# The last forgetting-attention pair sends three query tiles through DRAM, and the cross attention's first two query-weight loads queue behind the mixer's output weights

## The chip, the cores and the metric

The kernel runs on one core of one Trainium2 chip. The metric is the device time of one execution in microseconds (us), the median of several runs; lower is better. Engines are named as in the profile: PE is TensorE (matrix multiply; PEld is its weight load), DVE is VectorE, ACT is ScalarE, POOL is GpSimd, SP is SyncE, which here only issues DMAs; SPq is its queue.

## What is computed

One layer of a streaming encoder over 512 tokens of width 1024, in float32. A mixer runs four branches from one projection of the normalized input (differential attention, forgetting attention, a Conformer convolution, a short gated convolution), weighs them with sigmoid gates and projects the sum; then cross attention into 256 memory tokens; then a gated feed-forward block. The change touches the forgetting attention and the loading of the cross attention's query weights:

```python
def _forgetting_attention(q, k, v, log_f, t_pos):
    ...
    c = jnp.cumsum(log_f.astype(jnp.float32), axis=1)
    ...
        s = jnp.einsum('bqhd,bkhd->bhqk', q_blk, k, preferred_element_type=jnp.float32) * scale
        s = s + c_blk[..., None] - c_k[:, :, None, :]
        mask = t_pos[None, :] <= tq_blk[:, None]
        p = jax.nn.softmax(jnp.where(mask, s, -jnp.inf), axis=-1)
        return jnp.einsum('bhqk,bkhd->bqhd', p.astype(v.dtype), v)
...
        mixed = jnp.sum(gates * proj, axis=2) @ w_out[l]
        x = x + _rms_norm(mixed, norm_mix_post[l])
        hx = _rms_norm(x, norm_x_pre[l])
        ...
        xq = (hx @ w_xq[l]).reshape(B, S, X_HEADS, X_HEAD_DIM)
```

## The kernel before

**Arithmetic.** Every float32 product is made of three matmuls on a high part and a low part of each operand (`mm3`): high by high, high by low, low by high. So each weight block that arrives in the buffer `wr` is cast to `wh` on ACT (L201), and the rest is subtracted into `wl` on DVE (L202). `wr` has two buffers, `wh` and `wl` four each.

**Order of the work.** `run_blocks` takes a list of jobs in a fixed order (each is a weight load and a body of matmuls) and fetches the weights of later jobs ahead of the current one. The attention pieces are generators on a background queue (`bg`), which are advanced between the matmuls of the jobs. The instructions recorded in this way are then reordered on each engine by a list scheduler that works with estimated durations; an engine executes its own list strictly in order, and waits at an instruction until what that one needs has arrived.

**Forgetting attention.** The eight heads are worked in four pairs, `f_task(p, ...)` with p from 0 to 3. A pair has four steps for its query tiles of 128 tokens, tile 0 to tile 3, with 128, 256, 384 and 512 keys. In a step, POOL makes the forget bias, PE makes the scores of both heads into banks named `ps_sc` (`scores`), DVE adds the bias and takes the smallest (L1123; L1130 after the change), ACT takes the exponentials, and DVE and ACT scale them into the tile `e`, with queries on partitions. For the product with the values the keys have to be on partitions instead, in the tiles `pth` (high part) and `ptl` (low part). There are two ways to turn them:

- *through DRAM* (pairs 0 to 2): DVE transposes 32 x 32 squares (`turn_squares`, L857), SP writes the result to a DRAM tile `turned` (`put`, L862), and two more DMAs, one for each head, bring it back rearranged into `ptl` (`get`, L869). `split_in_place` then makes the high part on ACT (L875) and the low part on DVE (L876).
- *by the identity* (pair 3): PE transposes each 128 x 128 block against an identity matrix into a bank `ps_tr` (`to_keys_major`, L250), and `split` copies it from there with ACT (L164) and DVE (L165).

Tiles 0 and 1 together make the first half of the product with the values (`values(..., half=0)`), tiles 2 and 3 the second half; both accumulate into a bank `ps_av` for each head. The outcome goes into `y["f"]`. Around pair 3 the jobs on PE are the gate and branch blocks of the forgetting branch (`gate_blocks(1, "f", ...)`): gate blocks `ps_mm<-hth,wh` need nothing of the pair; the branch blocks `ps_mm<-y,wh` sum over four slices of `y["f"]`, of which the fourth is pair 3's.

**Mixer output and cross attention.** `mix_out_jobs` multiplies with seven products instead of eight and loads its weights (`load_parts`, L591) first into `wr`, then into a four-slot tile `wide`. The query weights of the cross attention, `in_w_xq`, are loaded by the job list's ordinary `load_weights` (L185) into `wr`; they are first needed when the mixer's output has been normalized.

Of the kernel before, what the change touches and what calls it, by code (L numbers as in the profile page):

```python
# [18 lines left out]
F32R = mybir.dt.float32r  # L19
# [6 lines left out]
P = 128  # L26
S = 512
# [11 lines left out]
HALF_SHIFT = 16  # L39
# [47 lines left out]
def hybrid_layer(ctx: ExitStack, tc: tile.TileContext, a: dict, out: bass.AP):  # L87
# [21 lines left out]
    def share_now(*among):  # L109
        vars(turn_of).update(n=1, among=among)  # L110
# [102 lines left out]
    steps_of = []  # L213
# [374 lines left out]
    def load_parts(raw, parts):  # L588
        c = 0
        for x in parts:  # L590
            SP.dma_start(raw[:, c:c + x.shape[1]], x)  # L591
            c += x.shape[1]

    def activation_sums(x, z, eng):
# [16 lines left out]
    def y8(dtype=F32R):  # L611
        return m2p.tile([P, 4, S], dtype, tag="y8", name="y8", bufs=2)
# [255 lines left out]
    def get(d, n, pt, local):  # L868
        SP.dma_start(part_of(pt[1], n, local).bitcast(F32), d.rearrange("(a j) (b x) -> (j b) a x", j=32, b=4))  # L869

    def split_in_place(n, pt, local):
        hi, lo = (part_of(x, n, local) for x in pt)
        raw = lo.bitcast(F32)
        with tc.issue_after(evacuations[0]):
            A.copy(hi, raw)  # L875
        V.tensor_tensor(lo, raw, hi.bitcast(F32), ALU.subtract)  # L876
# [21 lines left out]
    def pt_tiles():  # L898
        return tuple(m1p.tile([P, 2, 4, 4, 32], F32R, tag=n, name=n, bufs=2) for n in ("pth", "ptl"))
# [152 lines left out]

    def f_task(p, qk, v):
        f_steps[p] = 0
        far = p < 3
        while f_steps[p - 1] < 4:
            yield 0.0, 0.5
        ck = []
        for j in range(2):
            t = m1p.tile([P, S], F32, tag="ck", name="ck", bufs=2)  # L1060
            G.dma_start(t, crows[2 * p + j:2 * p + j + 1, :].rearrange("a s -> (a s)").partition_broadcast(P))
            ck.append(t)
        yield 0.0, 2.0 if p else 5.0
        es, pts, av, ready = {}, None, None, []
# [8 lines left out]
        for step in range(8 if far else 6):  # L1073
            if step in ((5, 7) if far else (3, 5)):
                if av is None:
                    av = [bank("av"), bank("av")]
                with tc.issue_after(steps_of[0]) if far else ExitStack():
                    for j in range(2):
                        hl = v[0][:, :, 2 * p + j]
                        values(av[j], lambda kt: ((hl[:, kt], 0), (hl[:, kt], 1)), pts[j],  # L1080
                               step // 2 - (2 if far else 1))
            while step == (3 if far else 2) and f_steps[p - 1] < 8:
                yield 0.0, 0.5
            f_steps[p] = step + 1
            cost = 0.0
            if step == 4:
                turn_ready()
            if far:
                for qt in SPLITS.get(step, ()):
                    for j in range(2):  # L1090
                        split_in_place(qt + 1, pts[j], qt % 2)
                    cost += 0.1 + 0.3 * qt
                for qt in GETS.get(step, ()):
                    if qt % 2 == 0:
                        pts = [pt_tiles() for _ in range(2)]
                    d = es.pop(qt)
                    for j in range(2):
                        get(d[:, j], qt + 1, pts[j], qt % 2)
            else:
                if step == 2:  # L1100
                    share_now("mm")
                for qt in {2: (0, 1), 3: (2,), 4: (3,)}.get(step, ()):
                    if qt % 2 == 0:
                        pts = [pt_tiles() for _ in range(2)]
                    e = es.pop(qt)
                    for j in range(2):
                        to_keys_major(e[:, j], qt + 1, pts[j], qt % 2)
                    cost += 0.4 + 0.3 * qt
            if step < 4:
                qt, w = step, (step + 1) * P  # L1110
                e = es[qt] = e4()
                st = m1p.tile([P, 8], F32, tag="st8", name="st8", bufs=4)
                for j in range(2):
                    head = 2 * p + j
                    bias = m1p.tile([P, S], F32, tag="fbias", name="fbias", bufs=2)

                    G.tensor_scalar(bias[:, :w], ck[j][:, :w], -1.0, cq[:, qt, head:head + 1],  # L1117
                                    ALU.mult, ALU.add)
                    G.affine_select(out=bias[:, w - P:w], in_=bias[:, w - P:w], pattern=[[-1, P]],
                                    compare_op=ALU.is_ge, fill=BIG, base=0, channel_multiplier=1)  # L1120
                    ps = bank("sc")
                    scores(ps, qk, j, qt * P, w)
                    low = V.tensor_tensor_reduce(e[:, j, :w], ps[:, :w], bias[:, :w], scale=-HD ** -0.5,  # L1123
                                                 scalar=3.0e38, op0=ALU.add, op1=ALU.min,
                                                 accum_out=st[:, j:j + 1])
# [12 lines left out]
                if far:  # L1138
                    ready.append((qt, e, w))
                    cost += 0.003 * w  # L1140
            yield cost, 6.5 if far and step == 5 else 4.5
        if "f" not in y:
            y["f"] = (y8(), y8())

        e = e4()
        for j in range(2):
            A.copy(e[0:HD, j], av[j][HD:P])
# [386 lines left out]
    def xq_jobs():  # L1534
        held = []
        for h in range(4):
            def body(hi, lo, h=h):
                held.append((hi, lo))

                def part(h, half):  # L1540
                    sl = slice(half * 256, (half + 1) * 256)
                    ps = bank()
                    (channel_major if h else by_pass)(ps, held[h], ns.hx, sl)
                    split(ps[:, sl], ns.xq[0][:, h, sl], ns.xq[1][:, h, sl])
                    bg.add(cross_task(h, half), f"x{half}")
                    bg.tick()

                if h == 0:
                    bg.drain("n0")
                part(h, 0)  # L1550
                if h == 3:
                    bg.drain("n1")
                    for g in range(4):
                        part(g, 1)
            yield *cols(w_xq, h * P), body, V, same, HALF_SHIFT

    def cross_values(half):
        bg.drain(f"x{half}")
# [333 lines left out]
```

## Time and profile before

| | |
|---|---|
| median of 3 runs | 1044.31 us (1044.2 to 1044.91) |
| the profiled execution, its own time | 1043.87 us |
| its span in the trace | 1042.1 us |
| TensorE clock granted | 0.999 |
| instructions | 14386 |
| PE, DVE, ACT, POOL busy | 1032.0, 816.3, 511.0, 158.5 us |

The busy times are unions of the intervals in which an engine had an instruction under way. Matmuls overlap: a new one starts before the one ahead has ended, so what one costs PE is read from the distance between starts and not from its duration. All times below are microseconds from the start of the span, unless ns is said.

### The profile page before, as it was taken

Reading aid. Unit: us, or ns where it says so; the run is one execution under the profiler, and the core shown is the slowest. Engines: PE = TensorE matmul, PEld = TensorE weight load, DVE = VectorE, ACT = ScalarE, POOL = GpSimd, SP = SyncE. Lnnn points to the kernel's source line nnn. Section 1 sums busy time; section 2 is a strip of 40 time slices with the busy share of each in tenths; the row PEclk is TensorE's granted clock in tenths of the full one; section 3 lists DMA queues with packets and bytes.
Section 4 is the critical chain, followed back from the end, with each engine's and each line's share of the span. In section 5 each row is a group of like instructions: output and inputs, shape, how many; then the busy total and the mean of one; then the engine's idle time right before and its main releaser. Section 6 shows DMA issues by size and latency. Waiting matters only on the chain.

```text
span 1042.1 us, 14386 instructions
## 1 busy us (share of the span) xinstructions
PE 1032.0 (99%) x5201; PEld 877.1 (84%) x5201; DVE 816.3 (78%) x1257; ACT 511.0 (49%) x838; POOL 158.5 (15%) x235
## 2 busy tenths in 40 slices
PE   9999999999999999999999999999999999999997
PEld 7888888888888988888888899998888888888886
DVE  7999999577788668878487898776767777667796
ACT  5322222376566365666444666655333433445662
POOL 4001000100020214353011031121112121111012
PEclk9999999999999999999999999999999999999999
DMA  8954333334534346766348744135577676625662
GB/s 268 311 159 104 102 101 101 84 99 115 148 104 126 90 130 169 199 175 161 104 136 284 246 127 121 59 123 181 187 241 235 211 234 210 218 81 186 212 218 82
DMA packets 190141, 167.79 MB, mean 161 GB/s; under 512 B 22079, under 2 KB 161708, under 8 KB 190069
## 3 DMA queue, kind: packets, MB, share of 16 engines
q1 hardware_dynamic: 181027, 135.11, 43.6%
q10 hardware_dynamic: 6482, 23.21, 6.2%
q0 software_dynamic: 2560, 8.54, 2.6%
q8 instruction: 41, 0.67, 0.3%
q14 instruction: 31, 0.25, 0.1%
HBM read 141.39 MB, written 25.44 MB: 160 GB/s over the span
## 4 chain that ended last, share of the span: by engine, by line
PE 96%; DMA 2%; DVE 1%; ACT 0%; issue 0%; POOL 0%; POOLq 0%; DVEq 0%; SPq 0%; ACTq 0%
PE ps_mm L244 46%; PE ps_av L244 30%; PE ps_tr L244 11%; PE ps_sc L244 7%; PE ps_tr L250 1%; DMA ptl<-turned 1%; PE ps_mm L462 1%; PE ps_av L462 1%; DMA turned<-e 0%; DMA xs<-in_x 0%; DVE e L857 0%; DVE e L939 0%; PE ps_tr L446 0%; DVE wl L202 0%; DVE o L1782 0%
## 5 line engine op out<-in xcount | busy, mean ns | idle before, releaser
L201 ACT CAST wh<-wr 128x1024 fp32r<-128x1024 f32 (+1 forms) x140 | 146.4, 1047 | 235.4 <-PE ps_mm L244 121.1
L202 DVE TENSOR_TENSOR wl<-wr,wh 128x1024 fp32r<-128x1024 f32 (+1 forms) x140 | 174.9, 1250 | 83.3 <-ACT wh L201 82.5
L244 PE MATMUL ps_mm<-hth,wh 128*128 128x512 f32 (+1 forms) x536 | 198.6, 378 | 0.0
L244 PE MATMUL ps_mm<-htl,wh 128*128 128x512 f32 (+1 forms) x536 | 198.4, 377 | 0.0
L244 PE MATMUL ps_mm<-hth,wl 128*128 128x512 f32 (+1 forms) x536 | 198.1, 377 | 0.0
L244 PE MATMUL ps_av<-htl,wh 128*128 128x512 f32 (+1 forms) x328 | 122.5, 373 | 0.0
L244 PE MATMUL ps_av<-hth,wh 128*128 128x512 f32 (+1 forms) x328 | 122.5, 374 | 0.0
L244 PE MATMUL ps_av<-hth,wl 128*128 128x512 f32 (+1 forms) x328 | 122.3, 373 | 0.0
L244 PEld LDWEIGHTS ps_mm<-hth,wl 128*128 128x128 f32 x536 | 99.1, 188 | 18.3
L244 PEld LDWEIGHTS ps_mm<-hth,wh 128*128 128x128 f32 x536 | 99.0, 188 | 18.1 <-ACT hth L164 0.3
L244 PEld LDWEIGHTS ps_mm<-htl,wh 128*128 128x128 f32 x536 | 98.9, 188 | 17.8
L697 DVE SCALAR_TENSOR_TENSOR y<-y,par,y 128x508 f32<-128x508 f32 (+29 forms) x120 | 82.6, 727 | 0.1
L244 PEld LDWEIGHTS ps_av<-hth,wh 128*128 128x128 f32 x328 | 61.6, 188 | 11.2 <-DVE e L1148 0.3
L244 PEld LDWEIGHTS ps_av<-hth,wl 128*128 128x128 f32 x328 | 61.6, 188 | 11.0
L244 PEld LDWEIGHTS ps_av<-htl,wh 128*128 128x128 f32 x328 | 61.6, 188 | 10.7
L1683 DVE TENSOR_TENSOR wl<-dw,wh 128x1024 fp32r<-128x1024 f32 x32 | 40.1, 1259 | 17.2 <-ACT wh L1682 17.1
L1682 ACT CAST wh<-dw 128x1024 fp32r<-128x1024 f32 x32 | 33.5, 1051 | 24.7 <-PE ps_tr L244 8.2
L1630 ACT ACTIVATE th<-c 128x512 f32<-128x512 f32 x22 | 13.9, 632 | 48.6 <-DVE c L624 48.6
L1117 POOL TENSOR_SCALAR fbias<-ck,cq 128x128 f32<-128x128 f32 (+3 forms) x32 | 24.2, 763 | 64.2 <-DVE st L1123 55.9
L624 DVE SCALAR_TENSOR_TENSOR c<-ps_mm,par,c 128x510 f32<-128x510 f32 (+1 forms) x44 | 32.7, 744 | 0.7
L244 PE MATMUL ps_tr<-htl,wh 128*128 128x512 f32 x80 | 31.7, 396 | 0.0
L244 PE MATMUL ps_tr<-hth,wh 128*128 128x512 f32 x80 | 31.6, 396 | 0.0
(514 smaller groups left out, 2242.2 us busy)
## 6 DMA issues: line engine op xcount, KB each, us to landing
wr<-in_w_up SPq DMA_DIRECT2D x44, 512.0 KB
wr<-in_w_in SPq DMA_DIRECT2D x38, 512.0 KB
wr<-in_w_gate SPq DMA_DIRECT2D x32, 512.0 KB
wp<-in_w_down ACTq DMA_DIRECT2D x22, 512.0 KB
sums<-wp ACTq DMA_DIRECT2D x22, 512.0 KB
dw<-sums SPq DMA_DIRECT2D x44, 256.0 KB
wr<-in_w_branch SPq DMA_DIRECT2D x16, 512.0 KB
wide<-in_w_out SPq DMA_DIRECT2D x12, 512.0 KB
```

The costliest lines, as they stand in the source:

```text
L201: last_weights[:] = [order(A.copy(hi, raw[:, :n])).ins, low.tensor_tensor(lo, raw[:, :n], hi.bitcast(F32), ALU.subtract).ins]
L202: low.tensor_tensor(lo, raw[:, :n], hi.bitcast(F32), ALU.subtract).ins]
L244: steps_of[:] = [PE.matmul(ps, lhs, rhs, start=start, stop=stop).ins]
L250: turns.append(PE.transpose(ps, x, ident[:n, :n]).ins)
L462: keep(PE.matmul(banks[c][:, :S // 2], w[p == 1][:, k, c * P:(c + 1) * P], ht[p == 2][:, i * 4 + k, :S // 2], start=(i, p, k) == (0, 0, 0) ...
L624: ins = V.scalar_tensor_tensor(dst[:, s:], src[:, :S - s], w(k), dst[:, s:], ALU.mult, ALU.add)
L697: ins = V.scalar_tensor_tensor(dst[:, s:], src[:, :S - s], pc("conv_dw", k * 4 + j), dst[:, s:], ALU.mult, ALU.add)
L1117: G.tensor_scalar(bias[:, :w], ck[j][:, :w], -1.0, cq[:, qt, head:head + 1], ALU.mult, ALU.add)
L1630: A.activation(th, c[:, 0], AF.Silu)
L1682: A.copy(hi, x)
L1683: V.tensor_tensor(lo, x, hi.bitcast(F32), ALU.subtract)
```

## The change

Pair 3 now sends its query tiles 0, 1 and 2 through DRAM, as the other pairs do, and turns only tile 3 by the identity. Tiles 0 and 1 return into a new tile `half` (`own_tiles`), which takes the buffer of an earlier pair's `qk`. Its steps are 0 to 6, with the first half of the values at step 5 and the second at step 6. `y["f"]` is allocated at the start of the first pair instead of at its end. In `xq_jobs`, the first two loads of `in_w_xq` are put behind the last DMA that `load_parts` has issued (`ns.part`), which is the last of the mixer's output weights.

```diff
     def load_parts(raw, parts):
...
-            SP.dma_start(raw[:, c:c + x.shape[1]], x)
+            ns.part = SP.dma_start(raw[:, c:c + x.shape[1]], x).ins
...
     def f_task(p, qk, v):
         f_steps[p] = 0
-        far = p < 3
+        last = p == 3
...
+        if "f" not in y:
+            y["f"] = (y8(), y8())
+        es, pts, av, ready = {}, {}, None, []
+        gets, splits, rests, ends = ({4: (2,)}, {4: (0, 1), 5: (2,)}, {3: 2.0}, (5, 6)) if last else (GETS, SPLITS, {5: 6.5}, (5, 7))
+
+        def fetch(qt):
+            d = es.pop(qt)
+            for j in range(2):
+                get(d[:, j], qt + 1, pts[qt // 2][j], qt % 2)
+
+        def own_tiles():
+
+            free = m1p.tile([P, 6, S], F32R, tag="qk", name="half", bufs=2)
+            return [tuple(free[:, 2 * j + i].rearrange("p (l a t i) -> p l a t i", l=2, a=4, t=2) for i in range(2))
+                    for j in range(2)]
...
-            if far:
-                for qt in SPLITS.get(step, ()):
...
-            else:
-                if step == 2:
-                    share_now("mm")
-                for qt in {2: (0, 1), 3: (2,), 4: (3,)}.get(step, ()):
...
-                        to_keys_major(e[:, j], qt + 1, pts[j], qt % 2)
+            for qt in splits.get(step, ()):
+                for j in range(2):
+                    split_in_place(qt + 1, pts[qt // 2][j], qt % 2)
+                cost += 0.1 + 0.3 * qt
+            for qt in gets.get(step, ()):
+                if qt % 2 == 0:
+                    pts[qt // 2] = [pt_tiles() for _ in range(2)]
+                fetch(qt)
+            if step == 4 and last:
+                share_now("mm")
+                e = es.pop(3)
+                for j in range(2):
+                    to_keys_major(e[:, j], 4, pts[1][j], 1)
+                cost += 1.3
...
-                if far:
+                if not last or qt < 3:
                     ready.append((qt, e, w))
                     cost += 0.003 * w
+                if last and qt == 2:
+                    pts[0] = own_tiles()
+                    fetch(0)
+                    fetch(1)
...
     def xq_jobs():
...
-            yield *cols(w_xq, h * P), body, V, same, HALF_SHIFT
+            def load(h=h):
+                with tc.issue_after(ns.part) if h < 2 else ExitStack():
+                    raw = load_raw(*cols(w_xq, h * P))
+                return split_weights(*raw, V, same, HALF_SHIFT)
+
+            yield load, None, body
```

What the scheduler makes of it is seen in the order of the instructions. On PE, before, pair 3's transposes of the third query tile stand between gate blocks (`ps_mm`) and pair 2's products with the values (`ps_av<-pth,v`):

```order
L244 MATMUL ps_av<-ptl,v 128x256
L244 MATMUL ps_av<-pth,v 128x128
L244 MATMUL ps_av<-ptl,v 128x128
L250 MATMUL ps_tr_4698<-ident,e 128x128 x3
L244 MATMUL ps_mm<-hth,wh 128x512
L244 MATMUL ps_mm<-htl,wh 128x512
L244 MATMUL ps_mm<-hth,wl 128x512
L244 MATMUL ps_av<-pth,v 128x256
```

After, on PE, only the eight transposes of the fourth tile are left. They stand behind 33 gate matmuls that follow the last scores, and the products with `half` (query tiles 0 and 1) stand among them:

```order
L244 MATMUL ps_mm<-hth,wl 128x512
L250 MATMUL ps_tr_4728<-ident,e 128x128 x4
L244 MATMUL ps_av<-half,v 128x256 x2
L250 MATMUL ps_tr_4721<-ident,e 128x128 x4
L244 MATMUL ps_av<-half,v 128x128 x2
L244 MATMUL ps_av<-half,v 128x256 x2
L244 MATMUL ps_av<-half,v 128x128 x2
L244 MATMUL ps_mm<-hth,wh 128x512
```

The second half of the values follows 15 matmuls later: six of the gate block and nine of a branch block. Twelve transposes have left PE's list.

On SP, before, nothing but weight loads follows the last two returns of pair 2 (128x4x128):

```order
L869 DMA ptl<-turned 128x4x128 x2
L185 DMA wr<-in_w_gate 128x8x128
L185 DMA wr<-in_w_branch 128x4x256
L185 DMA wr<-in_w_gate 128x8x128 x2
L185 DMA wr<-in_w_branch 128x4x256
```

After, on SP, three write-outs and six returns of pair 3 stand among them:

```order
L869 DMA ptl<-turned 128x4x128 x2
L862 DMA turned<-e 128x2x128
L185 DMA wr<-in_w_gate 128x8x128
L869 DMA half<-turned 128x4x32 x2
L862 DMA turned<-e 128x2x256
L185 DMA wr<-in_w_branch 128x4x256
L869 DMA half<-turned 128x4x64 x2
L862 DMA turned<-e 128x2x384
L869 DMA ptl<-turned 128x4x96 x2
L185 DMA wr<-in_w_gate 128x8x128 x2
```

A weight load that stood right behind another one now stands behind a return, which cannot be issued before the write-out ahead of it has landed.

Further on in SP's list, before, the first two loads of `in_w_xq` stand among the loads of the mixer's output weights (`wide`):

```order
L185 DMA wr<-in_w_xq 128x8x128
L591 DMA wide<-out_sums 128x512 x2
L591 DMA wide<-in_w_out 128x512
L591 DMA wide<-out_sums 128x512 x3
L591 DMA wide<-in_w_out 128x512
L591 DMA wide<-out_sums 128x512
L185 DMA wr<-in_w_xq 128x8x128
```

After, on SP, both stand behind the last of these and ahead of the cross attention's key and value weights (`mix<-in_w_xkv`):

```order
L591 DMA wide<-in_w_out 128x1024 x2
L591 DMA wide<-out_sums 128x512 x2
L185 DMA wr<-in_w_xq 128x8x128 x2
L185 DMA mix<-in_w_xkv 128x8x128 x3
L185 DMA mix<-in_w_xkv 128x2x512 x4
```

Both loads have moved past all the `wide` loads, and seven of the eight `in_w_xkv` loads now stand behind them. In the mixer's output projection and everything behind it PE's list is the same in both kernels, and so are those of DVE, ACT and POOL.

More of the change, by code (lines that the diff above doesn't have):

```diff
@@ L1072, in turn_ready @@
                 es[qt] = put(turned, w)
-        for step in range(8 if far else 6):
-            if step in ((5, 7) if far else (3, 5)):
+        for step in range(ends[1] + 1):
+            if step in ends:
                 if av is None:
                     av = [bank("av"), bank("av")]
-                with tc.issue_after(steps_of[0]) if far else ExitStack():
+                with tc.issue_after(steps_of[0]):
                     for j in range(2):
                         hl = v[0][:, :, 2 * p + j]
-                        values(av[j], lambda kt: ((hl[:, kt], 0), (hl[:, kt], 1)), pts[j],
-                               step // 2 - (2 if far else 1))
-            while step == (3 if far else 2) and f_steps[p - 1] < 8:
+                        half = ends.index(step)
+                        values(av[j], lambda kt: ((hl[:, kt], 0), (hl[:, kt], 1)), pts[half][j], half)
+            while step == (4 if last else 3) and f_steps[p - 1] < 8:
                 yield 0.0, 0.5
@@ L1087, in f_task @@
                 turn_ready()
-            if far:
-                for qt in SPLITS.get(step, ()):
[L1090 to L1098, printed above, removed]
-            else:
-                if step == 2:
-                    share_now("mm")
-                for qt in {2: (0, 1), 3: (2,), 4: (3,)}.get(step, ()):
[L1103 to L1106, printed above, removed]
-                        to_keys_major(e[:, j], qt + 1, pts[j], qt % 2)
-                    cost += 0.4 + 0.3 * qt
+            for qt in splits.get(step, ()):
[12 more added lines that the diff above has]
+                cost += 1.3
             if step < 4:
@@ L1137, in f_task @@
                 cost += 0.6 + 0.0038 * w
-                if far:
+                if not last or qt < 3:
                     ready.append((qt, e, w))
                     cost += 0.003 * w
-            yield cost, 6.5 if far and step == 5 else 4.5
-        if "f" not in y:
-            y["f"] = (y8(), y8())
+                if last and qt == 2:
+                    pts[0] = own_tiles()
+                    fetch(0)
+                    fetch(1)
+            yield cost, rests.get(step, 4.5)
         e = e4()
```

1 line of the change is left out of this document (removed).

## The prediction

> **What bounds the kernel now.** I read the page first: the busy shares, then the chain of work that ended last; then the view of who PE waited for.
>
> ```profile
> PE 1032.0 (99%) x5201; PEld 877.1 (84%) x5201; DVE 816.3 (78%) x1257; ACT 511.0 (49%) x838; POOL 158.5 (15%) x235
> PE 96%; DMA 2%; DVE 1%; ACT 0%; issue 0%; POOL 0%; POOLq 0%; DVEq 0%; SPq 0%; ACTq 0%
> PE ps_mm L403 <- DVE e L353: 1.3, 1, 1.3
> PE ps_tr L446 <- DVE nt L441: 1.0, 1, 1.0
> PE ps_av L244 <- ACT pth L875: 0.7, 1, 0.7
> ```
>
> PE is busy for 99% of the span and carries 96% of the chain. The last three rows are all the waits of PE that the trace names (in total, how often, the longest): two belong to the kernel's first lines, and the only one in the middle is 0.7 us, for the product with the values of an earlier task. So a change in the middle of this kernel is worth what it takes off PE's list, less what PE must newly wait for. Nothing that is saved on another engine counts by itself.
>
> **What leaves PE.** Tiles 0, 1 and 2 have 1, 2 and 3 blocks of keys, for two heads: 12 transposes. Their price is read from the starts of the rows around them in PE's timeline (start, duration, then the operation):
>
> ```profile
> 496.68 0.38 PE L250 MATMUL ps_tr<-ident,e 128*128 128x128 f32 x2
> 496.82 0.48 PE L244 MATMUL ps_mm<-hth,wh 128*128 128x512 f32 x1
> 497.14 0.40 PE L244 MATMUL ps_mm<-htl,wh 128*128 128x512 f32 x1
> 497.38 0.39 PE L244 MATMUL ps_mm<-hth,wl 128*128 128x512 f32 x1
> ...
> 503.04 0.52 PE L250 MATMUL ps_tr<-ident,e 128*128 128x128 f32 x3
> 503.31 0.48 PE L244 MATMUL ps_mm<-hth,wh 128*128 128x512 f32 x1
> ```
>
> Two transposes hold the next start back by 0.14 us, three by 0.27. The matmul right behind them takes 0.32 us to the next start (496.82 to 497.14), where the one after it takes 0.24 (to 497.38) and most of its kind 0.23, so a group costs some 0.09 us more for what follows it. The groups are: tile 0 with both heads in one place ahead of the scores, where I count 0.14 alone; tile 1 twice two, 2 x 0.23 = 0.46; tile 2 twice three, 2 x 0.36 = 0.72. In sum **1.3 us less on PE**. Tile 3's eight transposes stay.
>
> [...]
>
> **What DVE, ACT and SP get instead.** DVE loses six subtractions out of `ps_tr` and gets six transposes of squares and six subtractions in place; ACT keeps as many casts. SP gets three write-outs and six returns.
>
> ```profile
> 500.00:505.00 5.00, 5.00 (x30) 4.29 (x29) 2.12 (x3) 2.84 (x6) 0.00 (x0) 1.00 0.36 105
> 484.96 0.37 SPq L185 DMA_DIRECT2D wr<-in_w_gate  x1
> 498.98 1.04 ACT L201 CAST wh<-wr 128x1024 fp32r<-128x1024 f32 x1
> ```
>
> The first row is a stretch of 5 us in the view by stretches (PE, PEld, DVE, ACT, POOL busy, then clock, DMA share and GB/s): DVE is busy for 2.12 us of it and ACT for 2.84, so the added work lies beside PE's. What is queued behind the returns on SP are weight loads, and a return waits for its write-out first. The other two rows show why that is covered: with two buffers `wr`, the load issued at 484.96 is cast only at 498.98, 14 us later, and the cast weights then wait in one of four buffers. A load that comes 5 us late still comes in time. Without this cover each wait on SP would be PE time in full.
>
> **The new wait.** What can reach PE is the round trip of tiles 1 and 2, because the new order gives the products with them fixed places in PE's list. These rows give its parts: SP's issues of a write-out (L862) and of the return (L869) that waited for it; the first casts behind a return; and the steps around them:
>
> ```profile
> 395.46 1.06 SPq L862 DMA_DIRECT2D turned<-e  x1
> 399.07 0.92 SPq L869 DMA_DIRECT2D ptl<-turned  x2
> 400.51 0.36 SPq L862 DMA_DIRECT2D turned<-e  x1
> 403.25 0.91 SPq L869 DMA_DIRECT2D ptl<-turned  x2
> ...
> 460.44 0.37 SPq L862 DMA_DIRECT2D turned<-e  x1
> 461.42 0.62 SPq L869 DMA_DIRECT2D ptl<-turned  x1
> 465.74 0.91 SPq L869 DMA_DIRECT2D ptl<-turned  x2
> 402.27 0.58 ACT L875 CAST pth<-ptl 128x128 fp32r<-128x128 f32 x2 [2.77 <-DMA ptl<-turned]
> 466.50 0.75 ACT L875 CAST pth<-ptl 128x128 fp32r<-128x128 f32 x2 [1.41 <-DMA ptl<-turned]
> 465.82 1.60 DVE L857 STREAM_TRANSPOSE e<-e 128x384 f32<-128x384 f32 x2 [0.25 <-DMA turned<-e]
> 489.43 0.55 DVE L1123 CUSTOM_DVE_ANT_0 e<-ps_sc,fbias 128x384 f32<-128x384 f32 x1
> 492.90 0.65 POOL L1119 TENSOR_SCALAR_AFFINE_SELECT fbias<-fbias 128x128 f32<-128x128 f32 x2
> 492.25 1.15 PE L244 MATMUL ps_sc<-qk 128*128 128x512 f32 x4
> 493.24 0.40 PE L244 MATMUL ps_mm<-hth,wh 128*128 128x512 f32 x1
> ```
>
> A write-out takes 3.6 us (395.46 to 399.07), 2.7 (400.51 to 403.25) or 5.3 (460.44 to 465.74, with returns in flight beside it). A return takes about 3.2 us (399.07 to 402.27) or 5.1 (461.42 to 466.50).
>
> *When PE wants the tiles.* The scores of tile 3 start at 492.25 in before. Now 0.14 us of transposes are gone ahead of them and nine gate matmuls stand there instead of six, 0.23 each: 492.8. They last 0.99 (492.25 to 493.24), to 493.8. Then 33 gate matmuls at 0.23 take 7.5: tile 3's transposes at 501.3. The products with `half` need tile 1 at 501.7 (head 0) and 502.4 (head 1). Transposes and first half take about 1.4 and the 15 matmuls behind them 3.4: the second half starts at 506.2, and its second head at 507.0.
>
> *Tile 1.* Its squares are turned behind the 384-wide reductions, at about 490.4 to 491.6. Write-out 3.6: 495.2. Return 3.6, a little above the short one, since a weight load is issued between: 498.8. ACT then has in its list the cast for head 0, two copies out of `ps_av`, the scaling of tile 3 and the cast for head 1, together some 2.6 us, and DVE subtracts: head 1 is ready at about 502 against 502.4. With the short values it is a second and a half early, with the long ones (5.3 and 5.1, 3.2 us more) 2.8 us late.
>
> *Tile 2.* Its squares stand in DVE's list behind both reductions of tile 3's scores. POOL's bias is there at 493.55 and the second head's scores at 493.8; two reductions of some 0.7 and the scaling of tile 2 between them end at about 495.7. The squares take 1.6: 497.3. Write-out 3.6: 500.9. Return 3.6: 504.5, and 0.5 more for head 1. ACT casts and DVE subtracts head 0, then tile 3 of both heads out of `ps_tr`, then head 1: about 506.2 for head 0 and 507.4 for head 1, against 506.2 and 507.0. So I expect **0.4 us** of waiting here, and allow 0.2 us at tile 1's place, where the margin is half a microsecond. With the short values there is no wait; with the long ones it is 3.6 us here (what tile 1 has cost before that comes off it). I take the middle value because no weight load is issued in the 4 us ahead of tile 2's write-out.
>
> *Behind it.* The fourth slice of `y["f"]` is used 29 matmuls (6.6 us) after the second half. These rows are the first and the last step between, in before:
>
> ```profile
> 513.77 0.58 ACT L1147 COPY e<-ps_av 64x512 f32<-64x512 f32 x1 [1.47 <-PE ps_av L244]
> 517.99 0.69 DVE L165 TENSOR_TENSOR y<-e,y 128x512 fp32r<-128x512 f32 x1 [0.69 <-ACT y L164]
> ```
>
> 513.77 to 518.7 is 4.9 us, so this chain is covered with 1.7 us to spare.
>
> **The query weights.** Before, they are issued in the stage in which the transfers are fullest:
>
> ```profile
> 565.85 0.38 SPq L185 DMA_DIRECT2D wr<-in_w_xq  x1
> 582.14 0.80 SPq L591 DMA_DIRECT2D wide<-out_sums  x2
> 587.16 20.66 SPq L185 DMA_DIRECT2D mix<-in_w_xkv  x7
> 596.33 1.05 ACT L201 CAST wh<-mix 128x1024 fp32r<-128x1024 f32 x1 [1.45 <-PE ps_tr L244]
> 617.65 1.05 ACT L201 CAST wh<-wr 128x1024 fp32r<-128x1024 f32 x1 [2.06 <-PE ps_mm L244]
> 565.00:570.00 5.00, 5.00 (x23) 4.13 (x22) 4.86 (x9) 2.11 (x2) 0.00 (x0) 1.00 1.04 407
> ```
>
> In the last row the DMA engines are full, and PE is busy for 5 of 5 us all the same. So moving 1 MB out of this stage gains nothing on PE. After, the two loads are issued at about 583 and their first cast is at 617.65, 34 us later. The first of the seven key and value loads behind them, issued at 587.16, is cast at 596.33, and waits there for PE and not for its data. 1 MB at 407 GB/s is 2.6 us, issued 4 us ahead of it. I cost the move at nothing; its cover is the 9 us between that load and its cast.
>
> **The sum.** Against the profiled execution of 1043.87 us (span 1042.1 and 1.8 around it): -1.3 + 0.4 + 0.2 = -0.7, so 1043.2. The median of the runs, 1044.31, lies 0.4 above that execution; with the same difference I predict **1043.6 us**. About 0.2%, 2.1 us, is what a measurement of this kernel can tell from no change, and -0.7 is inside it.
>
> **Rivals.**
>
> *The round trip becomes the bound (slower).* Its place is PE's products with tiles 1 and 2. Its price is what a tile is ready after PE wants it. For it: tile 2 stands on SP behind four returns of its own pair and a weight load, and the trace has one write-out of 5.3 and one return of 5.1. Against it: pairs 0 to 2 work in the same way, and no wait of PE for their tiles is in the list above. It turns the sign from 1.3 us of waiting on and passes 0.2% at 3.4, that is with both parts at their longest: 1044.31 - 1.3 + 3.6 = 1046.6. Chance 0.13.
>
> [...] I give that 0.01.
>
> *A transpose costs PE its whole duration (faster).*
>
> ```profile
> L250 PE MATMUL ps_tr<-ident,e x24: 201/272/301, 383.4 to 511.4; 128*128 128x128 f32 x20, 8*128 8x8 f32 x4
> ```
>
> By the median of 272 ns it would be 12 x 0.272 = 3.3 us, and 1041.0 without new waits. Against it stand the starts, 0.14 us for two. Chance 0.06, gains that I don't see included.
>
> *Everything is covered.* With the short round trips PE waits for nothing: -1.3, 1043.0. That is no change by the bound either. So is the case in which both places wait 0.7 us longer than I think, 1044.3.
>
> **How the numbers follow.** No change by over 0.2%: the forecast 0.55, the covered case 0.15, the longer wait 0.10, together 0.80. Slower: 0.13 + 0.01 = 0.14. Faster: 0.06. The range goes from the covered case, less the 0.6 or so by which single runs differ (1044.2 to 1044.91), 1042.4, to just under the longest round trip, 1046.4.
>
> **What would show it.** Right: at L250 only eight transposes of `e` by 128x128 beside the four small ones, and waits of PE of some tenths between 501 and 508 us, in products with `half`, `pth` or `ptl`. Wrong: one wait of over 3 us there, with ACT waiting for the DMA into `ptl` ahead of it; a new wait of PE behind 560 us; or a span that falls by over 2 us.

## The result and the profile after

The changed kernel takes 1040.97 us (median of 8 runs, 1040.58 to 1042.13), the kernel before 1044.13 us (8 runs, 1043.29 to 1045.95): a ratio of 0.997, 95% interval 0.9961 to 0.998, that is 3.2 us less (2.1 to 4.1). A second measurement of both gave 1041.57 against 1044.22, ratio 0.997 (0.9959 to 0.9982). I had predicted 1043.6 us, between 1042.4 and 1046.4, and no change that a measurement could tell.

The page of the kernel after, with its span and busy times:

```profile
span 1039.2 us, 14390 instructions
PE 1029.6 (99%) x5189; PEld 876.3 (84%) x5189; DVE 819.5 (79%) x1263; ACT 510.9 (49%) x838; POOL 153.2 (15%) x235
```

The view of whom PE waited for (in total, how often, the longest):

```profile
PE ps_mm L403 <- DVE e L353: 1.3, 1, 1.3
PE ps_tr L446 <- DVE nt L441: 1.2, 1, 1.2
```

PE has twelve instructions less, and no wait in pair 3's stretch. The returns come in time. This is the order of the round trips in SP's timeline of after, with the first cast behind each return on ACT and DVE's last subtraction:

```profile
491.28 0.36 SPq L862 DMA_DIRECT2D turned<-e  x1
493.42 0.91 SPq L869 DMA_DIRECT2D half<-turned  x2
496.73 0.36 SPq L862 DMA_DIRECT2D turned<-e  x1
499.24 0.91 SPq L869 DMA_DIRECT2D ptl<-turned  x2
496.73 0.41 ACT L875 CAST half<-half 128x256 fp32r<-128x256 f32 x1 [0.69 <-DMA half<-turned]
503.35 0.51 ACT L875 CAST pth<-ptl 128x384 fp32r<-128x384 f32 x1 [2.03 <-DMA ptl<-turned]
505.59 0.55 DVE L876 TENSOR_TENSOR ptl<-ptl,pth 128x384 fp32r<-128x384 f32 x1
505.76 0.28 PE L244 MATMUL ps_av<-pth,v 128*128 128x256 f32 x1
506.65 0.33 PE L244 MATMUL ps_av<-pth,v 128*128 128x256 f32 x1
```

The write-outs take 2.1 us (491.28 to 493.42) and 2.5 (496.73 to 499.24), the returns 3.3 (493.42 to 496.73) and 4.1 (499.24 to 503.35). Head 1 of tile 2 is ready at 506.14, half a microsecond before PE comes to it at 506.65.

What the stretch gained is read from the stretch itself. It begins and ends with the same PE instruction in both kernels: 482.67 and 557.78 in before, 481.90 and 555.06 in after. The view by stretches (length, then PE, PEld, DVE, ACT, POOL busy, clock, DMA share, GB/s), first of before:

```profile
482.67:557.78 75.11, 75.01 (x360) 62.33 (x359) 54.46 (x86) 37.02 (x61) 11.97 (x16) 1.00 0.44 139
```

and of after:

```profile
481.90:555.06 73.16, 73.16 (x348) 61.42 (x347) 54.22 (x89) 35.22 (x59) 10.18 (x17) 1.00 0.59 177
```

The twelve transposes are gone, and the stretch is 1.95 us shorter. That alone is more than the 1.3 I counted, and it leaves about 1.2 us of the medians' difference outside this stretch. The experiments look for both.

### The profile page after: what moved, and what is told of

Same layout as the page of the kernel before. It is cut to its first block, busy times and chain, and to the rows that moved or that the text cites. A ratio compares the mean times of both kernels' runs of the same rounds, so it can differ in the third digit from the quotient of the medians.

```text
span 1039.2 us, 14390 instructions
## 1 busy us (share of the span) xinstructions
PE 1029.6 (99%) x5189; PEld 876.3 (84%) x5189; DVE 819.5 (79%) x1263; ACT 510.9 (49%) x838; POOL 153.2 (15%) x235
## 4 chain that ended last, share of the span: by engine, by line
PE 96%; DMA 2%; DVE 1%; ACT 0%; issue 0%; SPq 0%; POOL 0%; POOLq 0%; DVEq 0%; ACTq 0%
PE ps_mm L244 46%; PE ps_av L244 30%; PE ps_tr L244 11%; PE ps_sc L244 7%; PE ps_tr L250 1%; DMA turned<-e 1%; DMA ptl<-turned 1%; PE ps_mm L462 1%; PE ps_av L462 1%; DMA xs<-in_x 0%; DVE e L857 0%; DVE e L939 0%; DVE e L930 0%; PE ps_tr L446 0%; DVE wl L202 0%
## 5 line engine op out<-in xcount | busy, mean ns | idle before, releaser
L857 DVE STREAM_TRANSPOSE e<-e 128x128 f32<-128x128 f32 (+3 forms) x46 | 32.5, 729 | 0.2
L876 DVE TENSOR_TENSOR ptl<-ptl,pth 128x384 fp32r<-128x384 f32 (+3 forms) x42 | 20.7, 511 | 14.9 <-ACT pth L875 14.8
```

The source lines that it names most:

```text
L857: V.transpose(dst, src.rearrange("p (t j b) -> p b t j", b=4, j=32))
```

## The experiments

Each run's profile can be laid over the first profile of before: the same PE instruction, its start in one less its start in the other. This table, worked out from those starts, says by how much three stretches of PE's list are longer (+) or shorter (-) than in the first profile of before. The pair's stretch is the one above; 348 to 355 us holds the last value product of an earlier task (differential attention); 562 to 575 us is the first part of the mixer's output projection.

| kernel | 348 to 355 | pair 3's stretch | 562 to 575 | span |
|---|---|---|---|---|
| before, first | 0 | 0 | 0 | 1042.1 |
| before, second | -0.96 | +0.05 | +0.34 | 1042.1 |
| before, third | -0.39 | +0.02 | 0.00 | 1042.4 |
| before, fourth | -0.60 | 0.00 | +1.82 | 1044.3 |
| query weights only | +0.62 | +0.03 | +1.20 | 1044.3 |
| pair 3 only | -0.38 | -1.99 | +4.19 | 1044.0 |
| the change, first | -0.59 | -1.95 | 0.00 | 1039.2 |
| the change, second | -0.13 | -1.95 | 0.00 | 1040.1 |
| query weights on POOL's queue | -0.99 | -1.97 | 0.00 | 1039.2 |
| first query load ahead | -0.99 | -1.95 | +4.36 | 1043.7 |
| two tiles through DRAM | -0.31 | -1.18 | +0.01 | 1040.9 |
| tile 3's transposes twice | -0.66 | -1.11 | 0.00 | 1040.4 |
| memory tokens on POOL | -0.99 | 0.00 | 0.00 | 1041.2 |
| four tiles through DRAM | -0.95 | +2.52 | 0.00 | 1043.8 |

The first column varies by 0.96 us among the four profiles of before alone, by 1.6 among all six that leave pair 3 as it was, and by 0.9 among the eight with pair 3's change: the 0.57 us that my two first profiles differed there is chance. In the column of 562 to 575 us the 1.20 of the query weights alone comes from one wait of PE, 0.9 us for DVE's `ge`; it is taken up under "What is left of the difference". The second column repeats to within 0.05 us.

**Each part alone.** The change without its query-weight part:

```diff
...
-            yield load, None, body
+            yield *cols(w_xq, h * P), body, V, same, HALF_SHIFT
```

> The change without its query-weight part: w_xq is loaded where it was before; pair 3 as after. Theory 1 (all of the gain is made in pair 3's stretch of PE's list, 1.95 us by the two profiles there): 1.5 to 3 us below the kernel before, the same as the whole change within 0.5 us. Theory 2 (the earlier room in the transfers behind the mixer gives about 1 us of the 3.2): only 2 us below before, 1 us above the whole change. In the trace both expect no wait of PE between 480 and 560 us.

And the kernel before with the query-weight part alone (the opposite edit, with `ns.part` set in `load_parts`):

> Only the query-weight part on the kernel before: the first two w_xq loads go behind the last of the mixer's output weights. Theory 1: no difference, 0 +- 0.5 us, and PE's starts behind 560 us keep their distances to within 0.1 us. Theory 2: about 1 us below before.

Measured: pair 3 alone 1044.84 us, ratio to before 1.0001 (0.9992 to 1.001); the query weights alone 1044.66 us, ratio 1.0003 (0.9994 to 1.0011). Neither part gains anything; both together gain 3. So both theories fall, and the reason is at 568 us. Pair 3 alone does save 1.99 us in its stretch, but then loses 4.2. Whom PE waited for there, in pair 3 alone:

```profile
PE ps_mm L244 <- ACT wh L164: 1.4, 1, 1.4
PE ps_mm L244 <- DVE wl L165: 0.8, 1, 0.8
```

SP, ACT and PE in its timeline:

```profile
560.97 0.38 SPq L185 DMA_DIRECT2D wr<-in_w_xq  x1
561.41 1.36 SPq L591 DMA_DIRECT2D wide<-out_sums  x2
568.96 1.04 ACT L164 CAST wh<-wide 128x1024 fp32r<-128x1024 f32 x1 [7.37 <-DMA wide<-out_sums]
570.06 0.50 PE L244 MATMUL ps_mm<-wh,mix 128*128 128x512 f32 x1 [1.40 <-ACT wh L164]
571.32 0.80 PE L244 MATMUL ps_mm<-wl,mix 128*128 128x512 f32 x1 [0.76 <-DVE wl L165]
573.19 0.63 PE L244 MATMUL ps_mm<-wh,mix 128*128 128x512 f32 x1
573.62 0.63 PE L244 MATMUL ps_av<-wh,mix 128*128 128x512 f32 x1
```

and the same place on SP and ACT in the change as a whole:

```profile
554.80 0.80 SPq L591 DMA_DIRECT2D wide<-out_sums  x2
560.40 1.04 ACT L164 CAST wh<-wide 128x1024 fp32r<-128x1024 f32 x1
```

In the first, the query-weight load stands at the head of SP's list and can't go out before 560.97, because its buffer `wr` is in use until DVE has made the low part of the block in it. Eight `wide` loads stand behind it. In the whole change the first of them waits for PE's last gate matmul and goes out at 554.80; here it goes out 6.6 us later, at 561.41. ACT waits 7.37 us for it, and PE 1.4 and 0.8. The matmuls behind are then 0.43 us apart instead of 0.23 (573.19, 573.62).

Why the buffer comes free so late is seen in three rows: DVE's in before, then ACT's and DVE's in pair 3 alone:

```profile
555.05 1.22 DVE L165 TENSOR_TENSOR wl<-wr,wh 128x1024 fp32r<-128x1024 f32 x1
554.75 1.05 ACT L1318 CAST mth<-mn 128x1024 fp32r<-128x1024 f32 x1 [7.21 <-DMA mn<-turned_m]
559.72 2.54 DVE L165 TENSOR_TENSOR wl<-wr,wh 128x1024 fp32r<-128x1024 f32 x2
```

In before DVE makes this low part (of the mixer's second weight block) at 555.05, and the first query load goes out at 558.01. In the order that pair 3's change makes, the high and the low part of the cross attention's memory tokens (`mth` on ACT, `mtl` on DVE) stand ahead of it in the lists of these engines. They wait for a return from DRAM, ACT for 7.21 us, and the low part comes at 559.72. So "The change" is wrong where it calls the lists of DVE and ACT the same from the mixer's output projection on: these two steps have moved ahead of the mixer's second weight block. No run moves it alone; that it is the reason is read from the two traces.

**The queue or the bytes?** New theories: the load blocks SP's queue (Q), or its 1 MB takes transfer time from the `wide` loads (T). The first experiment issues the two loads on POOL's queue, without the new order behind `ns.part`:

```diff
-                with tc.issue_after(ns.part) if h < 2 else ExitStack():
-                    raw = load_raw(*cols(w_xq, h * P))
+                raw = load_raw(*cols(w_xq, h * P), queue=G if h < 2 else SP)
```

> The whole change, but the first two w_xq loads are issued by POOL's queue and wait for nothing but their buffer: they may move while the mixer's output weights arrive, and no longer stand ahead of them in SP's queue. Theory Q (in the run with pair 3 alone the first w_xq load waits in SP's queue for a buffer wr until 561 us, and the six wide loads behind it come 6 us late): no wait of PE between 560 and 580 us, the time is that of the whole change, about 3 us below before. Theory T (the 1 MB of w_xq takes transfer time, 2.6 us at 407 GB/s, away from the wide loads): PE still waits 1 to 2 us there, and the time is 2 us or more above the whole change.

The second puts only the second load behind the `wide` loads:

```diff
-                with tc.issue_after(ns.part) if h < 2 else ExitStack():
+                with tc.issue_after(ns.part) if h == 1 else ExitStack():
```

> The whole change, but the first w_xq load stands ahead of the wide loads in SP's queue again, as before; only the second is put behind them. Theory Q: the first load alone holds up the wide loads, so the wait of 2.2 us at 568 us and the slow matmuls behind it are there in full, and the time is that of pair 3 alone, about 1044.8. Theory T: half the bytes, half the loss, about 1043.

On POOL's queue: 1041.29 us, ratio to before 0.9974 (0.9963 to 0.9985), as the whole change. With the first load ahead: 1045.44 us, ratio 1.0015 (1.0006 to 1.0024). Theory Q holds; what theory T adds is bounded below. In the first kernel's timeline, POOL's issue of the load:

```profile
560.41 0.93 POOL L185 DMA_DIRECT2D wr<-in_w_xq  x1 [11.93 <-DMA wide<-out_sums]
```

and in its view by stretches the 14 us behind it:

```profile
562.00:576.00 14.00, 14.00 (x63) 11.59 (x62) 13.41 (x17) 7.70 (x8) 1.71 (x3) 1.00 1.04 363
```

Of the second kernel, the load's issue on SP:

```profile
561.35 0.38 SPq L185 DMA_DIRECT2D wr<-in_w_xq  x1
561.79 1.22 SPq L591 DMA_DIRECT2D wide<-out_sums  x2
```

On POOL the load goes out at 560.41, in pair 3 alone at 560.97, so its bytes travel at about the same time, but now behind the first `wide` loads (554.67) and beside the later ones. The DMA engines are full (1.04), and PE is nevertheless busy for 14.00 of 14 us. In the second kernel PE's two waits are there at their full length, 1.4 and 0.8 us: the first load alone makes them. That isn't the test of half the bytes that I took it for, because in pair 3 alone, too, the second load goes out only at 568.23, behind the eight `wide` loads.

What the first load's bytes add is bounded by the time from the issue of the first `wide` load to the cast behind it. It is 7.6 us in pair 3 alone (561.41 to 568.96) and at most 5.6 in the whole change (554.80 to 560.40). So of the 8.6 us by which this cast is late, 6.6 are the late issue and up to 2 can be transfer. In the order of before the load ahead made 0.2: 8.0 us in before with it (558.51 to 566.52), 7.8 with the query weights alone moved (560.61 to 568.37).

**What a transpose costs.** Two changes of the whole change. One turns tile 2 by the identity again:

```diff
-        gets, splits, rests, ends = ({4: (2,)}, {4: (0, 1), 5: (2,)}, {3: 2.0}, (5, 6)) if last else (GETS, SPLITS, {5: 6.5}, (5, 7))
+        gets, splits, rests, ends = ({}, {4: (0, 1)}, {3: 2.0}, (5, 6)) if last else (GETS, SPLITS, {5: 6.5}, (5, 7))
...
-                e = es.pop(3)
-                for j in range(2):
-                    to_keys_major(e[:, j], 4, pts[1][j], 1)
+                pts[1] = [pt_tiles() for _ in range(2)]
+                for qt in (2, 3):
+                    e = es.pop(qt)
+                    for j in range(2):
+                        to_keys_major(e[:, j], qt + 1, pts[1][j], qt % 2)
...
-                if not last or qt < 3:
+                if not last or qt < 2:
```

> Pair 3 sends only tiles 0 and 1 through DRAM; tile 2 is turned by the identity again, its two groups of three side by side behind the last scores instead of each between gate matmuls; everything else as in the whole change. Theory S (a transpose costs PE 0.09 us from start to start, and what the prediction missed is the step of 0.09 us behind each group among the gate matmuls and the gap of 0.4 us at 524 us): 6 x 0.09 + 0.1 = 0.6 us more in pair 3's stretch than the whole change, 73.8 us. Theory D (a transpose costs its whole 0.27 us): 1.6 us more, 74.8 us. The time: 0.6 or 1.6 us above the whole change, unless the earlier order of SP brings a new wait behind 550 us.

The other makes each transpose of tile 3 twice:

```diff
         for kt in range(n):
-            transpose(ps[:, kt * P:(kt + 1) * P], e[:, kt * P:(kt + 1) * P])
+            for _ in range(2):
+                transpose(ps[:, kt * P:(kt + 1) * P], e[:, kt * P:(kt + 1) * P])
```

> The whole change with each of tile 3's eight transposes made twice (the second overwrites the first with the same numbers). All sixteen stand in a row on PE. Theory S: 8 x 0.09 = 0.7 us more in pair 3's stretch. Theory D: 8 x 0.27 = 2.2 us more. Where the product with half needs tile 1 is 0.7 us later, so no wait is expected from either.

The stretch grows by 0.77 us for six transposes (-1.18 against -1.95) and by 0.84 us for eight: theory S, 0.105 us each in a row and little more behind a group. The medians, 1042.66 and 1042.17 us, stand 1.1 and 0.6 us above the 1041.57 of the whole change, which was measured in another series. PE's rows in the second:

```profile
500.88 1.91 PE L250 MATMUL ps_tr<-ident,e 128*128 128x128 f32 x16
502.54 1.13 PE L244 MATMUL ps_av<-half,v 128*128 128x256 f32 x8
```

Sixteen transposes hold the next start back by 1.66 us, 0.104 each, although each lasts 0.27.

**Tile 3 through DRAM as well.** The whole change, with the last eight transposes replaced in the same way and the second half of the values a step later:

```diff
-        gets, splits, rests, ends = ({4: (2,)}, {4: (0, 1), 5: (2,)}, {3: 2.0}, (5, 6)) if last else (GETS, SPLITS, {5: 6.5}, (5, 7))
+        gets, splits, rests, ends = ({4: (2,), 5: (3,)}, {4: (0, 1), 5: (2,), 6: (3,)}, {3: 2.0}, (5, 7)) if last else (GETS, SPLITS, {5: 6.5}, (5, 7))
...
```

> The whole change, and tile 3 goes through DRAM too: no transposes by the identity are left in pair 3, the second half of the values comes 24 gate matmuls later. Theory S (0.105 us for a transpose in a row, some tenths for steps behind groups): 8 x 0.105 = 0.8 us less in pair 3's stretch than the whole change if nothing waits, 72.3 us, and 1 us less time. Theory of the prediction (the new wait): tile 3's round trip ends the chain to the fourth slice of y["f"], PE waits for it in the branch blocks by 1 us or more, and nothing is gained.

1046.74 us, ratio to before 1.0033 (1.002 to 1.0045): 2.9 us slower than before (1043.8 in that series), and the stretch 4.5 us longer than in the whole change. Here PE waits. Its two longest waits in the timeline, each behind the rows that lead to it:

```profile
503.31 0.51 ACT L875 CAST pth<-ptl 128x384 fp32r<-128x384 f32 x1 [2.42 <-DMA ptl<-turned]
505.54 0.68 ACT L1169 ACTIVATE ge<-ps_mm,s_b_gate 128x512 f32<-128x512 f32 x1
506.27 0.50 PE L244 MATMUL ps_mm<-hth,wh 128*128 128x512 f32 x1 [1.62 <-ACT ge L1169]
505.27 1.10 SPq L869 DMA_DIRECT2D ptl<-turned  x2
511.59 0.62 ACT L875 CAST pth<-ptl 128x512 fp32r<-128x512 f32 x1 [5.37 <-DMA ptl<-turned]
517.09 0.73 PE L244 MATMUL ps_av<-y,wh 128*128 128x512 f32 x2 [1.97 <-DVE e L1152]
```

The first wait isn't made by tile 3. In this order ACT empties a gate bank (505.54), which PE needs, only after the casts behind the return of tile 2, for which it waits 2.42 us. The second is made by tile 3, whose return takes 6.3 us (505.27 to 511.59): the products with the values come late (PE waits 0.25 and 0.49 us for their casts), and a branch block can't start before DVE has taken their outcome out of `ps_av`. PE waits for that bank. I had expected it to wait for the fourth slice of `y["f"]`, but DVE finishes the slice at 519.12 while PE is at work.

**What is left of the difference.** Both kernels once more:

> The kernel before, unchanged, for a second profile. Theory A (the 0.57 us that the two profiles differ at 349.6 us, where PE waits for the cast behind a returned tile of an earlier pair, and the 0.2 us at the start, are chance): this wait comes out with another length than 0.7 us, differences of some tenths up and down, ratio 1.000. Theory B (they belong to the kernel before): the wait of 0.7 us is there again, and the span is 1042.1 +- 0.2.

> The changed kernel, unchanged, for a second profile. Theory A (chance): the wait at 349 us may show up here as well, and the span stands 1.7 to 3 us below that of a profile of before. Theory B (y["f"] taken at the start of the first pair changes what happens at 349 us): the wait is again absent. In pair 3's stretch both expect 73.2 us of PE against 75.1 before.

Theory A holds: the wait at 350 us is chance, and pair 3's stretch repeats. But the second profile of before lost 0.34 us behind 562, where no profile of the change with its order of SP lost anything. In before, DVE's subtraction into `mtl`, for the memory tokens of the cross attention, stands in DVE's list ahead of the low part of the mixer's third weight block and of `ge`, for which PE waits, and itself waits for a return from DRAM. In the change that round trip lies earlier, as its timeline shows (write-out, return, cast):

```profile
542.34 0.33 SPq L1312 DMA_DIRECT2D turned_m<-m_t  x1
547.21 0.37 SPq L1313 DMA_DIRECT2D mn<-turned_m  x1
553.66 1.05 ACT L1318 CAST mth<-mn 128x1024 fp32r<-128x1024 f32 x1 [6.59 <-DMA mn<-turned_m]
```

In the first profile of before its cast starts at 561.57, 8 us later. One experiment takes this out of before, by making both parts on POOL:

```diff
-            with tc.issue_after(evacuations[0]):
-                A.copy(hi, raw)
-            V.tensor_tensor(lo, raw, hi.bitcast(F32), ALU.subtract)
+            G.tensor_copy(hi, raw)
+            G.tensor_tensor(lo, raw, hi.bitcast(F32), ALU.subtract)
```

> The kernel before, but the memory tokens' high and low parts (the CAST into mth and the subtraction into mtl behind the return of the second 128 tokens) are made on POOL instead of ACT and DVE. PE's list stays the same. Theory M (part of the median gain beyond 1.95 us is that before sometimes waits some tenths at 566 us: DVE's mtl, which waits for that return, stands in DVE's list ahead of the weights' low parts and of ge, which PE needs; the whole change has the return 6 us ahead): no wait of PE at 566 us, and 0.3 to 1 us below before. Theory N (the rest is chance): 0 +- 0.4 us.

1043.11 us against 1043.8, ratio 0.9997 (0.9988 to 1.0006): it doesn't tell the theories apart. Two single profiles of before tell more:

> The kernel before, a third profile. Theory M: the step of PE's starts between 562 and 575 us is longer than in the first profile by 0.2 to 1.2 us, since DVE's mtl waits there for a return whose time varies. Theory N: it is as short as in the first profile, to within 0.1 us. Both: the wait at 350 us has again another length, from 0 to 1.6 us.

> The kernel before, a fourth profile, with the same expectations: by theory M 0.2 to 1.2 us more between 562 and 575 us than in the first profile, by theory N within 0.1 us of it; at 350 us a wait of another length.

The third profile lost nothing there, the fourth 1.82 us. In that one DVE's steps for the memory tokens come 2.3 us late. In its timeline the return's issue, the two steps behind it, and PE:

```profile
559.95 0.37 SPq L1305 DMA_DIRECT2D mn<-turned_m  x1
563.86 1.05 ACT L1310 CAST mth<-mn 128x1024 fp32r<-128x1024 f32 x1 [5.78 <-DMA mn<-turned_m]
564.94 1.23 DVE L1311 TENSOR_TENSOR mtl<-mn,mth 128x1024 fp32r<-128x1024 f32 x1 [5.29 <-ACT mth L1310]
567.95 0.50 PE L244 MATMUL ps_mm<-wh,mix 128*128 128x512 f32 x1 [1.52 <-DVE ge L1177]
```

The delay begins 20 us earlier, at the return of the first 128 memory tokens. It is issued at 535.87 in the first profile and at 535.97 in the fourth; the cast behind it, in the first and in the fourth:

```profile
541.27 1.05 ACT L1310 CAST mth<-mn 128x1024 fp32r<-128x1024 f32 x1 [1.26 <-DMA m_t<-in_mem]
543.52 1.05 ACT L1310 CAST mth<-mn 128x1024 fp32r<-128x1024 f32 x1 [3.40 <-DMA mn<-turned_m]
```

In the first the last thing that the cast waited for was another DMA, so the return itself may have landed still earlier. It took at least 2 us longer in the fourth, and all that follows it on ACT and DVE came as much later. In two other profiles it was the write-out of the second 128 tokens that took longer: 5.2 us in the second profile of before and 5.9 with the query weights alone, against 4.3 in the first.

So before has a wait at this place that is 0, 0.34, 0 and 1.82 us in four profiles, 0.5 on average, and the query weights alone, which leave pair 3 as it was, 1.20 in one; the six profiles with pair 3's change in which the weights come in time have none. The mechanism of theory M is there; its size is not the 0.2 to 1.2 us that I expected of each profile. 1.95 and 0.5 are 2.5 us, within the interval of 2.1 to 4.1, but four profiles give a rough average. Why a round trip takes longer in one execution than in another, and whether the rest of the difference is chance, stays open. None of the kernels is faster than the change by more than its runs differ.

## Why the prediction was wrong

I had forecast 0.7 us less, and 3.2 were measured. Of the 2.5 us between them 0.65 is the term of the transposes, 0.6 the waits that did not come, and 1.2 lies outside pair 3's stretch.

- **Transposes, -1.3.** The way of pricing was right, by starts: 0.105 us each, not 0.27. The full duration of 272 ns would have made the eight doubled ones cost 2.2 us, and they cost 0.84. The term was too small: the stretch gained 1.95. By the groups' starts with the step behind each, all transposes took some 2.2 us in before and 0.8 in after, about 1.45 less. Of the 0.14 beyond my 1.3, some 0.09 is the step behind tile 0's group, for which I had counted nothing: the scores behind it take 0.26 us to the next start, where others of their width take 0.17. Another 0.38 was a wait that before's list of waits doesn't show. In before's PE timeline:

```profile
523.38 0.39 PE L244 MATMUL ps_mm<-y,wl 128*128 128x512 f32 x1
523.83 0.39 PE L244 MATMUL ps_av<-y,wl 128*128 128x512 f32 x1
524.06 0.39 PE L244 MATMUL ps_av<-hth,wl 128*128 128x512 f32 x1
524.55 0.73 PE L244 MATMUL ps_mm<-y,wh 128*128 128x512 f32 x2
```

  The step from 524.06 to 524.55 is 0.26 too long, and 0.12 more lies in the next. DVE empties the bank `ps_mm` only after its last product, issued at 523.38; its step runs from 523.81 to 524.50. In after's order no such step is there. What is left, 0.12 us, is about what one more step of PE in before, from 517.36 to 517.69, is too long; the weight load ahead of it, at 517.35, waited 0.28 us for DVE's `e`.
- **The wait for tile 2, +0.4, and for tile 1, +0.2.** This step failed in its size. I took 3.6 us for a write-out, from a row of an earlier pair; they took 2.1 and 2.5. The returns, 3.3 and 4.1, were near the 3.6 assumed. (The "second and a half" by which tile 1 was to be early is microseconds.) With the shorter write-outs, head 1 of tile 2 came 0.5 us ahead of PE and not 0.4 behind it, and nothing waited. That PE's place in the list is near its edge was right: sending tile 3 the same way made the stretch 4.5 us longer.
- **The chain to `y["f"]`, nothing.** Right, nothing waits there with three tiles.
- **The query weights, nothing.** This step failed in its mechanism. I looked at the bytes, found the DMA engines full with PE busy, and named a cover at 596 us. The load that I showed, at 565.85, is the second one; the first stands ahead of the `wide` loads (558.01), and what it waits for I didn't ask. Against the kernel before, the move alone does cost and gain nothing, as I said. But I priced it against before's order and not against the order that the other half of the change makes. There ACT and DVE wait for the memory tokens ahead of the mixer's weights, the first query load would have waited for its buffer and held up the `wide` loads until 561 us, 4.2 us of PE; in the medians, 1044.84 against 1041.57, it was worth 3.3 us. Pair 3's gain exists only because this load was moved. That nothing is the right entry in my sum all the same is luck: I left out a loss that pair 3's order brings and the move that takes it away, and the two cancel.
- **A time read from one profile.** I took PE's stretch behind 560 us as it was in one execution. In others before loses up to 1.8 us there, and the change doesn't. By the average of four profiles that is some 0.5 of the 1.2 us by which the median moved beyond the stretch.
- **The rivals.** "Everything is covered" had the waits right, and 1043.0. "The round trip becomes the bound" did not come true with three tiles; with four it did. The 0.01 in the sum for slower stands for a return many times as long as a write-out. No run shows one: pair 3's returns took 3.3 and 4.1 us in the change, behind write-outs of 2.1 and 2.5, and the longest, with four tiles through DRAM, 6.3.

Of the signs that I named, the eight transposes are there, the waits of some tenths are not, and one of the signs of being wrong came true: the span fell by 2.9 us, more than 2.

## What to carry to other kernels

A change with two parts is priced by asking of each part what it does in the order that the other one makes; each of these two was worth nothing without the other. On a queue that issues in order, as SP's does here (560.97 and 561.41 above), look first not at the bytes of a transfer but at what it waits for and which transfers stand behind it: moving one load behind its neighbours, or to another queue, saved 3 us here (1041.57 and 1041.29 against 1044.84), where full DMA engines (1.04) beside a busy PE had made it look worth nothing. And a stretch with a return from DRAM close to PE's need should be looked at in several profiles before its wait is called zero: in four profiles of before one such wait was 0, 0.34, 0 and 1.82 us.

## What the runs showed of the hardware

In pair 3 alone PE waited for 1.4 and for 0.8 us, with a matmul between the two, and in the 2 us ahead of 571 it was busy for 0.50. The granted clock then fell to 0.50 during the second wait. It stayed there for some 3.4 us, 571 to 574.4, an estimate from the 0.51, 0.50, 0.50 and 0.78 of the last four rows. The view by stretches of one microsecond each:

```profile
569.00:570.00 1.00, 0.00 (x0) 0.00 (x0) 0.00 (x0) 1.00 (x1) 0.00 (x0) 1.00 0.80 209
570.00:571.00 1.00, 0.50 (x1) 0.19 (x1) 0.96 (x1) 0.01 (x1) 0.00 (x0) 1.00 1.01 322
571.00:572.00 1.00, 0.68 (x2) 0.59 (x3) 0.97 (x3) 0.65 (x1) 0.00 (x0) 0.51 1.05 406
572.00:573.00 1.00, 1.00 (x4) 0.81 (x3) 0.96 (x3) 1.00 (x2) 0.00 (x0) 0.50 1.07 383
573.00:574.00 1.00, 1.00 (x3) 0.76 (x3) 1.00 (x2) 1.00 (x3) 0.00 (x0) 0.50 1.13 356
574.00:575.00 1.00, 1.00 (x5) 0.78 (x4) 1.00 (x2) 1.00 (x3) 0.00 (x0) 0.78 1.12 367
```

Waits of 2.2 us so cost 4.2 (+4.19 in the table). With the first query load ahead the waits are 1.4 and 0.8 us too, and the stretch is 4.36 us longer. Behind a single wait of 1.5 us (the fourth profile of before) the clock was 1.00 over 562 to 576, and behind two of 1.6 and 2.0 us, 11 us apart (four tiles through DRAM), it was 1.00 in every stretch of 5 us from 500 to 545. What decides whether the clock falls, no run here shows.
